# The S5 mixer's kernel product, a pair of inputs to a quarter of TensorE's columns, and its transposes at places of their own

## The chip, the cores and the metric

The kernel runs on one core of a Trainium2 chip. The metric is the device time of one execution in microseconds (us), the median of several runs. A core has a matrix engine (TensorE, in the profile PE), a vector engine (VectorE, DVE), a scalar engine (ScalarE, ACT), GpSimd (POOL) and SyncE (SP), which here only issues DMA transfers. Each engine works through its own queue of instructions in order; semaphores make one wait for another. PE reads its operands from SBUF, 128 partitions wide, and writes its results into PSUM; the output's partitions are the columns of PE.

## The reference, cut to what matters

One inference step of a two-layer streaming encoder, float32, model width 1024, 1024 prompt positions and 64 sample positions. Layer 0 mixes tokens by sliding-window attention, layer 1 by an S5 state-space model; after each mixer stands a gated ConvFFN of width 2816. The state-space model has 64 groups of 16 channels, each with 64 complex states:

```python
lbar_re, lbar_im = mag * cos(li * dt), mag * sin(li * dt)        # mag = exp(lr * dt)
bbar_re = cr[..., None] * br - ci[..., None] * bi                # and bbar_im
h[t] = lbar * h[t - 1] + bbar @ u[t]                             # complex, for each group
y = einsum('blgp,gip->blgi', sr, c_re) - einsum('blgp,gip->blgi', si, c_im) + d_skip * u
z = gelu(y);  out = (z @ w_glu + b_glu)[..., :D] * sigmoid((z @ w_glu + b_glu)[..., D:])
```

The kernel computes this over blocks of eight positions. For that it needs, for every group, the short convolution kernel K[t] = Re(C λ^t B) for t = 0 to 7 (16 × 16 channels each). This is the mixer's kernel product.

## The kernel before, in words

All large products (projections, FFN, GLU) go through `mm3` (L221): weight and input are each split into a high and a low part, and three matmuls (L223, L224, L225) add up in PSUM. A block of outputs is 128 channels by 384, 384 or 320 positions, summed over eight slices of the model width, 24 matmuls in a row. The tiles come from a framework that gives every instruction a priority in the order in which the program is written (`tc.cur_priority` counts up) and then forms each engine's queue by these priorities and a timeline of its own. `later(n)` (L118) writes the instructions inside it with a priority n lower than their place. `order(x, y)` (L112) makes x follow y in the queue.

The matrices of the state-space model are prepared while PE works on the first FFN's up-projection: `ffn` calls `aside` (L443) after each step, and in the first 32 of these (SIDE, L27) it advances the generator `ssm_prep` (L1098) by one piece under `later(LOW)` (LOW is 1500, L26). The pieces are `ssm_small`, and then for each of eight chunks q (four pairs of groups each) `ssm_chunk(q)` in two pieces and `ssm_toeplitz(q)`. A chunk:

- computes `ct` (C times powers of λ; DVE), `oc` (ACT) and `w` (B times powers of λ; six DVE instructions by `cmul`, of which L887 is the last),
- puts each group's B into `bd_` (ACT, L1048), a tile filled with zeros once,
- multiplies on PE, in float32: `kps` (L1062), eight matmuls for four pairs g and two parts c (real and imaginary). Before the change `bd_[:, g, c]` is 128 columns wide with the pair's 32 columns at 32 g and zeros beside them, and all eight matmuls add up in the same 128 × 128 of PSUM,
- takes `kps` out on DVE to `kt` (L1066, L1067), which goes to DRAM (`kd`); `ssm_toeplitz` reads it from there, rearranges it and writes it into `prm`,
- transposes `w` on PE in two groups of four, one for each part c (`wps`, L1073), takes each group out on ACT (`b3`, L1074) and writes it into `prm` too; last, POOL computes the tables `tab`.

`kps` and the transposes of part 0 share one PSUM tile (`sm0`); the transposes of part 1 have `sm1`. So the part-0 group waits until DVE has read `kps`; the part-1 group does not, and waits at most for `w` and for ACT's earlier reading. All of `kps` and `wps` are ordered behind the last product that was written when the chunk was (`behind`, L1059).

Around this, DVE works for the up-projection: it takes products out of PSUM (L411), runs the convolution (L419 to L421 on ACT and DVE), and in these turns forms sums of gated activations for the down-projection (`jt`, L370 to L373, written to DRAM as `td`).

The mixer itself, `ssm` (from L1196), comes after the FFN. It goes through 32 pairs in batches, mostly of two: `p` = U by `pm` on PE (L1249), tables on ACT, a scan on DVE (L1297), then two products into `po` (L1309 with `pm` and U, L1315 with the scan's result). `pm` is a pair of `prm`'s pairs, loaded by SP (L1213). U is the input, in four pieces of 16 groups (L1186, two DMAs each); the third and fourth stand in buffers that earlier tiles held, the third in that of the FFN's last block, so that it must wait until this block has been written out to `x1` (the spill, L1552). ACT takes `po` out and every second batch writes it to DRAM as `yd` (L1330); SP reads it back as `yf` (L1335), and ACT applies the GELU to it as `z` (L1350). SP's queue holds the spill, and all `pm`, U and `yf`, in one row.

Of the kernel before, what the change touches and what calls it, by code (L numbers as in the profile page):

```python
# [8 lines left out]
F32 = mybir.dt.float32  # L9
F32R = mybir.dt.float32r  # L10
I32 = mybir.dt.int32
AF = mybir.ActivationFunctionType
# [3 lines left out]
P = 128  # L16
# [27 lines left out]
class Core:  # L44
# [72 lines left out]
    @contextmanager  # L117
    def later(self, n):  # L118

        p = self.tc.cur_priority  # L120
        self.tc.cur_priority = p + n
        yield
        self.tc.cur_priority = p

    @contextmanager
    def boundary(self, nsq=2):
# [84 lines left out]
    behind = ()  # L211
# [680 lines left out]
    def ssm_small(self):  # L892

        nc, a = self.nc, self.a
# [5 lines left out]
        sm = self.prep.tile([P, 1024], F32, name="sm0", tag="sm").rearrange("p (a q) -> p a q", a=32)  # L900
# [79 lines left out]
        c, s = cs, sn  # L980
        for k in range(10):
# [8 lines left out]
            c, s = (ph[:, 0, k - 2], ph[:, 1, k - 2]) if k > 1 else (ta[:, 8], ta[:, 9])  # L990
# [3 lines left out]
        for t, n, p0 in ((self.tq[:, :, 0:32], 16, 0), (self.tp[:, :, 18:36], 9, 4)):  # L994
            t = t.rearrange("p q (c k) -> p q c k", c=2)
            V.memset(t[:, :, 0, 0:1], 1.0)
            V.memset(t[:, :, 1, 0:1], 0.0)
            w, k = 1, p0
            while w < n:
# [3 lines left out]
                m = [m[:, i, :NPR * u].rearrange("p (q j) -> p q j", j=u) for i in range(2)]  # L1003
                self.cmul(V, [t[:, :, i, w:w + u] for i in range(2)], [t[:, :, i, 0:u] for i in range(2)], y, m)
                w, k = w + u, k + 1
        self.bd_ = self.prep.tile([P, 4, 2, P], F32, name="bd", tag="sm")
        V.memset(self.bd_, 0.0)
        self.dv = self.prep.tile([P, 24], F32, name="dv")
        nc.sync.dma_start(self.dv[:, 16:], a["s_d"])
# [6 lines left out]
    def ssm_chunk(self, q):  # L1016

        nc, a = self.nc, self.a
        G, V = nc.gpsimd, nc.vector
        gs = slice(4 * q, 4 * q + 4)  # L1020
        if q == 0:
            z = self.pt([P, 8, 112], "z0")
            G.memset(z, 0.0)
            nc.sync.dma_start(self.kd[:, 0:7].rearrange("(b p) t i -> p b (t i)", p=P), z)
        two = lambda t, o, n: (t[:, gs, o:o + n], t[:, gs, o + n:o + 2 * n])
        (ac, as_), (bbr, bbi), (cr, ci) = (two(self.tq, o, 16) for o in (0, 32, 64))
        (pr, pi), (bc, bs) = two(self.tp, 0, 9), two(self.tp, 18, 9)

        ct = self.pt([P, 4, 2, 9, 16], "ct")
        m = self.pm2()  # L1030
        m1, m2 = (m[:, i].rearrange("p (g t i) -> p g t i", t=9, i=16) for i in range(2))
        wide = lambda x: x[:, :, None, :].to_broadcast([P, 4, 9, 16])
        tall = lambda x: x[:, :, :, None].to_broadcast([P, 4, 9, 16])
        V.tensor_mul(m1, wide(cr), tall(pr))
        V.tensor_mul(m2, wide(ci), tall(pi))
        V.tensor_sub(ct[:, :, 0], m1, m2)
        V.tensor_mul(m1, wide(cr), tall(pi))
        V.tensor_mul(m2, wide(ci), tall(pr))
        V.scalar_tensor_tensor(ct[:, :, 1], m1, -1.0, m2, op0=ALU.mult, op1=ALU.subtract)
        oc = self.pt([P, 4, 2, 16, 8], "oc")  # L1040
        for c in range(2):
            nc.scalar.activation(oc[:, :, c], ct[:, :, c, 1:9].rearrange("p g t i -> p g i t"), AF.Copy)
        nc.sync.dma_start(self.prm[:, gs, OC:OC + 256], oc.rearrange("p g c i t -> p g (c i t)"))

        for e, r in enumerate((slice(0, 64), slice(64, 128))):
            o = self.bd_[r, 0, 0, 16 * e:16 * e + 1]
            o = bass.AP(tensor=o.tensor, offset=o.offset, ap=[o.ap[0], [2 * P + 32, 4], [P, 2], [1, 16]])
            nc.scalar.activation(o, self.tq[r, gs, 32:64].rearrange("p g (c j) -> p g c j", c=2), AF.Copy)  # L1048

        w = self.pt([P, 4, 2, 16, 8], "w")  # L1050
        m = self.pm2()
        m = [m[:, i, :512].rearrange("p (g j s) -> p g j s", j=16, s=8) for i in range(2)]
        row = lambda x: x[:, :, :, None].to_broadcast([P, 4, 16, 8])
        pwr = lambda x: x[:, :, None, 0:8].to_broadcast([P, 4, 16, 8])
        self.cmul(V, (w[:, :, 0], w[:, :, 1]), (row(bbr), row(bbi)), (pwr(pr), pwr(pi)), m)
        yield

        kps = self.sm_ps("kps", 0)
        behind = self.last_mm  # L1059
        for g in range(4):  # L1060
            for c in range(2):
                x = nc.tensor.matmul(kps[:, :P], self.bd_[:, g, c], ct[:, g, c, 0:8].rearrange("p t i -> p (t i)"),  # L1062
                                     start=g + c == 0, stop=g + c == 4)
                self.order(x, behind)
        kt = self.prep.tile([P, P], F32, name="kt")
        V.scalar_tensor_tensor(kt[:, 0:16], self.dv[:, :16], self.dv[:, 16 + q:17 + q], kps[:, 0:16], op0=ALU.mult, op1=ALU.add)  # L1066
        V.tensor_copy(kt[:, 16:], kps[:, 16:P])  # L1067
        nc.sync.dma_start(self.kd[q * P:q * P + P, 7:].rearrange("j t i -> j (t i)"), kt)
        b3 = self.pt([P, 4, 2, P], "b3")
        for c in range(2):  # L1070
            wps = self.sm_ps("wps", c)
            for g in range(4):
                self.order(nc.tensor.transpose(wps[:, g * P:g * P + P], w[:, g, c].rearrange("p j s -> p (j s)"), self.ident), behind)  # L1073
            nc.scalar.activation(b3[:, :, c], wps.rearrange("p (g n) -> p g n", g=4), AF.Copy)  # L1074
        nc.sync.dma_start(self.prm[:, gs, OW:OW + 256], b3.rearrange("p g c n -> p g (c n)"))

        tab = self.pt([P, 4, 2, 144], "tab")
        m = self.pm2()
        m = [m[:, i].rearrange("p (g b a) -> p g b a", b=9, a=16) for i in range(2)]
        v = lambda i: tab[:, :, i].rearrange("p g (b a) -> p g b a", a=16)  # L1080
        self.cmul(G, (v(0), v(1)), (wide(ac), wide(as_)), (tall(bc), tall(bs)), m)
        G.tensor_copy(tab[:, :, :, 129:138], tab[:, :, :, 0:9])
        for c, o in enumerate((OCO, OSI)):
            nc.gpsimd.dma_start(self.prm[:, gs, o:o + 138], tab[:, :, c, 0:138])
# [515 lines left out]
```

## Time and profile before

| | us |
| --- | --- |
| median of 3 runs | 2254.64 |
| lowest and highest | 2249.07, 2256.94 |
| profiled execution, its own time | 2264.88 |
| its span in the trace | 2263.1 |
| PE busy | 2201.7 (97%) |
| DVE busy | 1688.5 (75%) |
| ACT busy | 1019.2 (45%) |
| eight chunks' `kps` and transposes on PE | 615.6 to 898.9 |
| the state-space model's batches, first and last `pm` issued | 1181.2 to 1278.7 |

The span is the time from the first to the last instruction in the trace of one profiled execution. A row of the timeline gives the start in us, how long the instruction was there, the engine, the line, what was written from what, the shape and how many of the kind stood in a row; in brackets stands how long the engine was idle before it, and for whom it waited. Matmuls are pipelined: a row's duration overlaps the next, so what one costs is read from the distance between the starts. Of each float32 matmul the trace has two records, of the split products (fp32r) one. In a shape such as 128*64 128x256 the first pair is rows by columns of PE.

### The profile page before, as it was taken

Reading aid. Unit: us, or ns where it says so; the run is one execution under the profiler, and the core shown is the slowest. Engines: PE = TensorE matmul, PEld = TensorE weight load, DVE = VectorE, ACT = ScalarE, POOL = GpSimd, SP = SyncE. Lnnn points to the kernel's source line nnn. Section 1 sums busy time; section 2 is a strip of 40 time slices with the busy share of each in tenths; the row PEclk is TensorE's granted clock in tenths of the full one; section 3 lists DMA queues with packets and bytes.
Section 4 is the critical chain, followed back from the end, with each engine's and each line's share of the span. In section 5 each row is a group of like instructions: output and inputs, shape, how many; then the busy total and the mean of one; then the engine's idle time right before and its main releaser. Section 6 shows DMA issues by size and latency. Waiting matters only on the chain. (4 is left out here: it accounts for less than half of the span.)

```text
span 2263.1 us, 36074 instructions
## 1 busy us (share of the span) xinstructions
PE 2201.7 (97%) x13875; PEld 2122.4 (94%) x13875; DVE 1688.5 (75%) x2954; ACT 1019.2 (45%) x1839; POOL 415.2 (18%) x474
## 2 busy tenths in 40 slices
PE   8999999999999999999998899999999999999997
PEld 8987789999999999999996799999999999989997
DVE  8677647989877777667767855588997787686764
ACT  5255747422333343455534641263544444355543
POOL 5322004200042423000200034352011011100000
PEclk9999999999999999999998999999999999999999
DMA  5100014656345565887749888652266577578773
GB/s 195 37 21 29 16 65 151 242 191 211 107 138 185 178 203 179 259 288 222 227 164 339 262 286 300 234 166 74 96 233 218 213 287 258 193 250 278 222 256 99
DMA packets 208124, 428.48 MB, mean 189 GB/s; under 512 B 23312, under 2 KB 114224, under 8 KB 205008
## 3 DMA queue, kind: packets, MB, share of 16 engines
q1 hardware_dynamic: 175648, 326.56, 44.0%
q0 software_dynamic: 23984, 95.12, 11.6%
q10 hardware_dynamic: 8320, 4.49, 0.9%
q8 instruction: 109, 1.79, 0.3%
q14 instruction: 63, 0.52, 0.1%
HBM read 297.75 MB, written 128.37 MB: 188 GB/s over the span
## 5 line engine op out<-in xcount | busy, mean ns | idle before, releaser
L223 PE MATMUL mm<-hl,whl 128*128 128x384 f32 (+1 forms) x1960 | 643.8, 329 | 7.7 <-DVE hl L306 3.1
L225 PE MATMUL mm<-hh,whl 128*128 128x384 f32 (+1 forms) x1960 | 641.1, 328 | 2.3 <-DVE whl L216 2.3
L224 PE MATMUL mm<-hh,whl 128*128 128x384 f32 (+1 forms) x1960 | 642.2, 328 | 0.0
L223 PEld LDWEIGHTS mm<-hl,whl 128*128 128x128 f32 x1960 | 368.4, 188 | 10.8 <-DVE hl L306 4.5
L225 PEld LDWEIGHTS mm<-hh,whl 128*128 128x128 f32 x1960 | 368.4, 188 | 2.9 <-DVE whl L216 2.9
L224 PEld LDWEIGHTS mm<-hh,whl 128*128 128x128 f32 x1960 | 368.7, 188 | 0.0
L216 ACT ACTIVATE whl<-raw 128x1024 fp32r<-128x1024 f32 x202 | 212.9, 1058 | 339.1 <-PE mm L225 176.4
L216 DVE TENSOR_TENSOR whl<-raw,whl 128x1024 fp32r<-128x1024 f32 x202 | 254.4, 1263 | 96.7 <-ACT whl L216 96.2
L223 PE MATMUL mm<-gt,whl 128*128 128x384 f32 (+1 forms) x968 | 318.5, 329 | 7.9 <-DVE y L613 3.6
L225 PE MATMUL mm<-gt,whl 128*128 128x384 f32 (+1 forms) x968 | 316.9, 328 | 0.7 <-DVE whl L216 0.7
L224 PE MATMUL mm<-gt,whl 128*128 128x384 f32 (+1 forms) x968 | 317.3, 328 | 0.0
L223 PEld LDWEIGHTS mm<-gt,whl 128*128 128x128 f32 x968 | 182.9, 189 | 10.5 <-DVE y L613 4.9
L225 PEld LDWEIGHTS mm<-gt,whl 128*128 128x128 f32 x968 | 182.7, 189 | 1.0 <-DVE whl L216 1.0
L224 PEld LDWEIGHTS mm<-gt,whl 128*128 128x128 f32 x968 | 182.8, 189 | 0.0
L194 DVE TENSOR_TENSOR whl<-raw,whl 128x1024 fp32r<-128x1024 f32 x84 | 96.3, 1153 | 73.0 <-ACT whl L193 72.4
L193 ACT ACTIVATE whl<-raw 128x1024 fp32r<-128x1024 f32 x84 | 82.6, 986 | 126.8 <-DMA raw<-sd 51.0
L419 ACT ACTIVATE t<-u,ppt 128x1090 f32<-128x1090 f32 x88 | 114.2, 1298 | 50.6 <-DVE u L521 24.6
L420 DVE SCALAR_TENSOR_TENSOR t<-u,ppt,t 128x1090 f32<-128x1090 f32 x88 | 123.6, 1406 | 9.8 <-ACT t L419 9.1
L421 DVE SCALAR_TENSOR_TENSOR t<-u,ppt,t 128x1090 f32<-128x1090 f32 x88 | 123.4, 1403 | 0.4
L563 DVE TENSOR_TENSOR gt<-gr,gt 128x768 fp32r<-128x768 f32 (+2 forms) x106 | 90.2, 880 | 10.7 <-ACT gt L562 10.1
L331 POOL TENSOR_TENSOR y<-y,xl 128x768 f32<-128x768 f32 (+1 forms) x16 | 31.3, 1954 | 354.0 <-DVE y L328 288.0
L562 ACT ACTIVATE gt<-gr 128x768 fp32r<-128x768 f32 (+2 forms) x106 | 78.3, 771 | 39.5 <-DMA gr<-gd 30.2
(390 smaller groups left out, 4181.0 us busy)
## 6 DMA issues: line engine op xcount, KB each, us to landing
raw<-in_w_up SPq DMA_DIRECT2D x88, 512.0 KB, 4.3
raw<-in_w_down SPq DMA_DIRECT2D x74, 512.0 KB, 4.5
raw<-sd SPq DMA_DIRECT2D x40, 512.0 KB, 4.6
sj<-in_w_up POOLq DMA_DIRECT2D x68, 256.0 KB, 6.4
su<-sj POOLq DMA_DIRECT2D x34, 512.0 KB, 5.8
raw<-su SPq DMA_DIRECT2D x34, 512.0 KB, 4.8
pm<-prm SPq DMA_DIRECT2D x32, 522.0 KB, 8.2
gr<-td SPq DMA_DIRECT2D x40, 384.0 KB, 5.9
```

What stands on the lines that cost most here:

```text
L193: nc.scalar.activation(w[:, 0], raw, AF.Copy)
L194: nc.vector.tensor_sub(w[:, 1], raw, w[:, 0].bitcast(F32))
L216: x = nc.scalar.activation(w[:, 0], raw, AF.Copy), nc.vector.tensor_sub(w[:, 1], raw, w[:, 0].bitcast(F32))
L223: nc.tensor.matmul(out, w[:, 0, sl], xl, start=start, stop=False)
L224: nc.tensor.matmul(out, w[:, 0, sl], xh, start=False, stop=False)
L225: self.last_mm = nc.tensor.matmul(out, w[:, 1, sl], xh, start=False, stop=stop)
L331: x = by[q].tensor_add(yq, yq, xs[q])
L419: nc.scalar.activation(t, u[:, 0:T + 2], AF.Identity, bias=cb(m), scale=cw(0, m))
L420: nc.vector.scalar_tensor_tensor(t, u[:, 1:T + 3], cw(1, m), t, op0=ALU.mult, op1=ALU.add)
L421: self.last_conv = nc.vector.scalar_tensor_tensor(t, u[:, 2:T + 4], cw(2, m), t, op0=ALU.mult, op1=ALU.add)
L562: nc.scalar.activation(x[:, 0, u], raw, AF.Copy)
L563: nc.vector.tensor_sub(x[:, 1, u], raw, x[:, 0, u].bitcast(F32))
```

## The change

`bd_` becomes 32 columns wide: each pair's weights alone, without the zeros for the other pairs. Each of the eight `kps` matmuls writes only its pair's 32 partitions of PSUM, so that a pair takes a quarter of PE's columns. The loop over the parts c is now the outer one, and each pair adds up over c by itself. A new context manager `due(p)` writes an instruction with the priority p itself instead of one relative to its place. The eight `kps` all get the priority that the place of the first has; the transposes of part 1 get that plus 12, and are now written first; those of part 0 get it plus 50.

```diff
+    @contextmanager
+    def due(self, p):
+
+        q = self.tc.cur_priority
+        self.tc.cur_priority = p
+        yield
+        self.tc.cur_priority = q
...
-        self.bd_ = self.prep.tile([P, 4, 2, P], F32, name="bd", tag="sm")
+        self.bd_ = self.prep.tile([P, 4, 2, 32], F32, name="bd", tag="sm")
...
         for e, r in enumerate((slice(0, 64), slice(64, 128))):
-            o = self.bd_[r, 0, 0, 16 * e:16 * e + 1]
-            o = bass.AP(tensor=o.tensor, offset=o.offset, ap=[o.ap[0], [2 * P + 32, 4], [P, 2], [1, 16]])
-            nc.scalar.activation(o, self.tq[r, gs, 32:64].rearrange("p g (c j) -> p g c j", c=2), AF.Copy)
+            nc.scalar.activation(self.bd_[r, :, :, 16 * e:16 * e + 16], self.tq[r, gs, 32:64].rearrange("p g (c j) -> p g c j", c=2), AF.Copy)
...
-        for g in range(4):
-            for c in range(2):
-                x = nc.tensor.matmul(kps[:, :P], self.bd_[:, g, c], ct[:, g, c, 0:8].rearrange("p t i -> p (t i)"),
-                                     start=g + c == 0, stop=g + c == 4)
+
+        due = self.tc.cur_priority
+        for c in range(2):
+            for g in range(4):
+                with self.due(due):
+                    x = nc.tensor.matmul(kps[32 * g:32 * g + 32, :P], self.bd_[:, g, c], ct[:, g, c, 0:8].rearrange("p t i -> p (t i)"),
+                                         start=c == 0, stop=c == 1)
                 self.order(x, behind)
...
-        for c in range(2):
+        for c in (1, 0):
             wps = self.sm_ps("wps", c)
             for g in range(4):
-                self.order(nc.tensor.transpose(wps[:, g * P:g * P + P], w[:, g, c].rearrange("p j s -> p (j s)"), self.ident), behind)
+                with self.due(due + (50 if c == 0 else 12)):
+                    x = nc.tensor.transpose(wps[:, g * P:g * P + P], w[:, g, c].rearrange("p j s -> p (j s)"), self.ident)
+                self.order(x, behind)
```

What this does to the queues is seen in their order. PE's queue, chunk 0 in the up-projection, before (`mm` are the FFN's products, `whl` its weights; the eight `kps` go on alternating with products, and nine products after the last stands the first transpose):

```order
L224 MATMUL mm<-hh,whl 128x384
L225 MATMUL mm<-hh,whl 128x384
L1062 MATMUL kps<-ct,bd 128x128
L223 MATMUL mm<-hl,whl 128x320
L1062 MATMUL kps<-ct,bd 128x128
L224 MATMUL mm<-hh,whl 128x320
L1062 MATMUL kps<-ct,bd 128x128
L225 MATMUL mm<-hh,whl 128x320
```

The same place now, where the lines stand some eight to ten further down:

```order
L232 MATMUL mm<-hh,whl 128x384
L233 MATMUL mm<-hh,whl 128x384
L1071 MATMUL kps<-ct,bd 32x128
L231 MATMUL mm<-hl,whl 128x320
L1071 MATMUL kps<-ct,bd 32x128 x7
L232 MATMUL mm<-hh,whl 128x320
L233 MATMUL mm<-hh,whl 128x320
```

One `kps` still has a product behind it; the other seven stand together. Eleven products after them comes one transpose of part 1, a product, and the other three; before, the group's four stood alternating with products. The part-0 group stands some twenty products further on, likewise one, a product, three; before, in one run of four, seven products after the other group.

DVE's queue, the fifth chunk (`w` its last product, `kt` the way out of `kps`, `jt` and `u` the FFN's), before:

```order
L887 TENSOR_TENSOR w<-m 128x4x128
L371 TENSOR_TENSOR jt<-jt 128x384
L411 TENSOR_TENSOR u<-rb,mm 128x384
L372 TENSOR_TENSOR jt<-jt 128x384
L373 TENSOR_TENSOR jt<-jt 128x384
L1066 SCALAR_TENSOR_TENSOR kt<-dv,kps 128x16
L1067 COPY kt<-kps 128x112
L411 TENSOR_TENSOR u<-rb,mm 128x256
```

And now:

```order
L895 TENSOR_TENSOR w<-m 128x4x128
L379 TENSOR_TENSOR jt<-jt 128x384
L419 TENSOR_TENSOR u<-rb,mm 128x384
L380 TENSOR_TENSOR jt<-jt 128x384
L1075 SCALAR_TENSOR_TENSOR kt<-dv,kps 128x16
L1076 COPY kt<-kps 128x112
L381 TENSOR_TENSOR jt<-jt 128x384
L419 TENSOR_TENSOR u<-rb,mm 128x256
```

`kt` stands ahead of the last of the sums instead of behind it. The same holds in the third and the seventh chunk; in the eighth it moved ahead of an L411; the others are unchanged. `w` keeps its place.

SP's queue in the state-space model's stage, where the change touches no line, before (`pm` are loads of pairs of `prm`, U_11629 the third piece of the input and U_11888 the fourth, `x1` the spill):

```order
L1213 DMA pm_11601<-prm_289 128x1044 x2
L1552 DMA x1_91<-y_10702 1024x1x320
L1213 DMA pm_11691<-prm_289 128x1044 x2
L1186 DMA U_11629<-hd_10753 128x8x137 x2
L1213 DMA pm_11748<-prm_289 128x1044 x2
L1335 DMA yf_11747<-yd_11538 128x1096
L1213 DMA pm_11804<-prm_289 128x1044 x2
L1213 DMA pm_11861<-prm_289 128x1044 x2
L1186 DMA U_11888<-hd_10753 128x8x137 x2
L1335 DMA yf_11860<-yd_11538 128x1096
L1213 DMA pm_11932<-prm_289 128x1044 x2
```

And now:

```order
L1224 DMA pm_11601<-prm_289 128x1044 x2
L1563 DMA x1_91<-y_10702 1024x1x320
L1197 DMA U_11629<-hd_10753 128x8x137 x2
L1224 DMA pm_11691<-prm_289 128x1044 x2
L1224 DMA pm_11748<-prm_289 128x1044 x2
L1346 DMA yf_11747<-yd_11538 128x1096
L1224 DMA pm_11804<-prm_289 128x1044 x2
L1224 DMA pm_11861<-prm_289 128x1044 x2
L1346 DMA yf_11860<-yd_11538 128x1096
L1197 DMA U_11888<-hd_10753 128x8x137 x2
L1224 DMA pm_11932<-prm_289 128x1044 x2
```

The third piece of the input stands ahead of the load of pairs 12 and 13 (pm_11691), and the second `yf` ahead of the fourth piece. On PE two of this stage's L1309 groups stand behind the next batch's `p` instead of ahead of it. ACT's and POOL's queues change by single neighbouring places.

## Prediction

> **What bounds the kernel now.** The page first: section 1 says which engine fills the span.
>
> ```profile
> span 2263.1 us, 36074 instructions
> PE 2201.7 (97%) x13875; PEld 2122.4 (94%) x13875; DVE 1688.5 (75%) x2954; ACT 1019.2 (45%) x1839; POOL 415.2 (18%) x474
> ```
>
> TensorE (PE) is busy for 97% of the span. So an instruction taken from its queue shortens the time by what it holds that queue, and a wait taken from another engine only where PE waits for it. Next the list of PE's waits (total, times, longest), of which three belong to the places that the change touches.
>
> ```profile
> PE p L1249 <- DMA pm<-prm: 4.8, 5, 2.1
> ...
> PE wps L1073 <- DVE kt L1067: 4.4, 3, 1.7
> ...
> PE wps L1073 <- DVE w L887: 2.9, 3, 1.2
> ```
>
> The two L1073 rows are the chunk's transposes, which wait for VectorE (DVE): one group for `w`, the other for `kt`, whose read frees the PSUM tile they share with `kps`. The L1249 row is in the SSM stage. Then the timeline of PE in chunk 0, where it is not disturbed by waits.
>
> ```profile
> 615.62 0.38 PE L1062 MATMUL kps<-ct,bd 128*128 128x128 f32 x2
> ...
> 618.58 0.31 PE L225 MATMUL mm<-hh,whl 128*128 128x320 f32 x1
> ...
> 619.75 0.27 PE L1073 MATMUL wps<-ident,w 128*128 128x128 f32 x1
> ...
> 620.78 0.30 PE L225 MATMUL mm<-hh,whl 128*128 128x320 f32 x1
> ```
>
> From 618.58 to 619.75 eight products of 320 columns run: 1.17 us, 0.146 each from start to start. From 615.62 to 618.58 eight `kps` and eight products alternate: 2.96 − 1.17 = 1.79 us for the eight `kps`, 0.22 each; each is two records, so 0.11 a record. From 619.75 to 620.78 four transposes alternate with four products: 1.03 − 4 × 0.146 = 0.45, 0.11 each. At full width an instruction costs its own columns and nothing for standing between others.
>
> **The kps in quarters.** Each chunk's eight `kps` now write 32 partitions each, so they use 32 of the columns of PE. No row of before shows four quarters. The nearest shows halves: the attention's `po`, 64 columns wide, among full-width products.
>
> ```profile
> 232.55 0.31 PE L225 MATMUL go<-oh,whl 128*128 128x320 f32 x1
> 232.79 0.65 PE L796 MATMUL po<-ptT,vt 128*64 128x256 f32 x4
> 233.37 0.33 PE L789 MATMUL tps<-ident,ptT 128*128 128x128 f32 x1
> ...
> 261.11 1.09 PE L796 MATMUL po<-ptT,vt 128*64 128x256 f32 x8
> 262.13 0.41 PE L223 MATMUL go<-ol,whl 128*128 128x320 f32 x1
> 262.38 0.31 PE L224 MATMUL go<-oh,whl 128*128 128x320 f32 x1
> ```
>
> Four records take 0.58 (232.79 to 233.37), eight take 1.02: 0.44 for four more, 0.11 each, although a record of 256 columns alone should take twice the 0.11 of one of 128. So two halves run at once, 0.22 a pair, and 0.58 − 0.44 = 0.14 a run is left over. The last full-width product ahead holds 0.24 instead of 0.146 (232.55 to 232.79), the first behind 0.25 (262.13 to 262.38): 0.09 and 0.10 more. Leaving full width and coming back costs 0.14 + 0.09 + 0.10 = 0.33 us an excursion.
>
> By the order, the eight do not stand in one run: one comes first, then a product, then seven. That is two excursions. The lone one costs 2 × 0.11 + 0.33 = 0.55. Of the seven, no quarter holds more than two (four records): 4 × 0.11 + 0.33 = 0.77 if all four quarters run at once. Together 1.32 against 1.79: −0.47 a chunk, **−3.8 us** for eight. If only two run at once, the seven take 0.88 + 0.33 = 1.21, together 1.76: −0.2 in all. If none, 14 × 0.11 + 0.33 = 1.87, together 2.42: +5.0 in all. I take four at once, since the halves show nothing but full concurrency.
>
> The rule that speaks against this change: the Trainium skill, TensorEngine Tiling (Array Packing), section Key Properties, says that changing the tiling mode (not just the tile) drains TensorE. It names no price; the trace agrees, with 0.33 an excursion, and without it the term would be 1.79 − 0.66 = 1.13 a chunk, −9.0 in all. The Trainium skill, TensorE: Matmul & The Clock Gate, Part 3 (packing small matmuls), measures 2.38× for three column tiles instead of 3×; by that an estimate of the seven's 0.44 is 0.55, and the term −2.9.
>
> **The waits of the transposes.** Before, the group that waits for `w` stood behind 16 products and the eight `kps`, 16 × 0.146 + 1.79 = 4.13 us after the chunk's first `kps`. Now 12 products and the shorter `kps` are ahead of it: 1.75 + 1.32 = 3.07. `w` does not come sooner by that. Two of the eight chunks, the fifth (PE, then DVE) and the last:
>
> ```profile
> 772.36 0.38 PE L1062 MATMUL kps<-ct,bd 128*128 128x128 f32 x2
> 781.65 0.63 PE L1073 MATMUL wps<-ident,w 128*128 128x128 f32 x4 [1.44 <-DVE kt L1067]
> 777.13 0.69 DVE L887 TENSOR_TENSOR w<-m 128x512 f32<-128x512 f32 x1
> 779.77 1.41 DVE L373 TENSOR_TENSOR jt<-jt 128x384 f32<-128x384 f32 x1
> 781.11 0.22 DVE L1066 SCALAR_TENSOR_TENSOR kt<-dv,kps 128x16 f32<-128x16 f32 x1
> ...
> 890.61 0.38 PE L1062 MATMUL kps<-ct,bd 128*128 128x128 f32 x2
> 895.54 0.68 DVE L887 TENSOR_TENSOR w<-m 128x512 f32<-128x512 f32 x1
> ```
>
> In the fifth, `w` ends at 777.82, 5.5 after the first `kps`; in the last at 896.22, 5.6 after. Over the eight chunks the same subtraction gives −6.5, 2.5, 2.3, 4.8, 5.5, 3.6, 3.8, 5.6. Set against 4.13 (the last chunk's products are partly 384 wide, its place 4.4) the waits are 0.7, 1.4 and 1.3, in all 3.4; set against 3.1 (in the last chunk 4.7, since its order changes more) they are 1.7, 2.4, 0.6, 0.7 and 1.0, in all 6.4: **+3.0 us**. These are delays of the queue, a little more than the 2.9 of idle time in the waits' list.
>
> The group that waits for `kt` moves the other way, from six to eight products after the other group to some twenty. And in the third, fifth and seventh chunk DVE now does `kt` ahead of L373 (1.41 us, above) instead of behind it. Its delays before were 1.85, 1.7 and 1.4 (second, fifth, seventh chunk; 4.9 in all). The last two go, and so does what they would have hidden; the second chunk's falls to 1.1, as PE is about 0.75 later there. **−3.9 us.** What is late next is L373 in three chunks, by the 0.35 of `kt`; its `jt` goes out to DRAM for the down-projection, which has not begun. `bd` written by simpler ScalarE instructions: as many, off the path, 0. The smaller fill with zeros (DVE) runs once, ahead of the first chunk: 0.
>
> Sum in the up-projection: −3.8 + 3.0 − 3.9 = −4.7. With no concurrency of quarters PE comes later, the `w` delays are 1.9 and the `kt` delays 0: +5.0 − 1.5 − 4.9 = −1.4.
>
> **The SSM stage.** The changed priorities also move two loads on SP's queue there; nothing is added. These are SP's issues before, then PE's `p` batches, then ACT's `z`.
>
> ```profile
> DMA packets 23980, 37.55 MB, mean 289 GB/s; under 512 B 1040, under 2 KB 17424, under 8 KB 23968
> ...
> U<-hd SPq DMA_DIRECT2D x8, 548.0 KB, 9.7
> ```
> ```profile
> 1212.13 0.52 SPq L1552 DMA_DIRECT2D x<-y  x1
> 1215.06 4.60 SPq L1213 DMA_DIRECT2D pm<-prm  x2
> 1225.87 1.11 SPq L1186 DMA_DIRECT2D U<-hd  x2
> 1227.10 5.55 SPq L1213 DMA_DIRECT2D pm<-prm  x2
> ...
> 1237.87 1.80 SPq L1186 DMA_DIRECT2D U<-hd  x2
> 1247.57 0.33 SPq L1335 DMA_DIRECT2D yf<-yd  x1
> ```
> ```profile
> 1226.68 1.16 PE L1249 MATMUL p<-U,pm 128*64 128x137 f32 x16
> ...
> 1231.77 1.16 PE L1249 MATMUL p<-U,pm 128*64 128x137 f32 x16
> ...
> 1239.32 0.69 PE L1249 MATMUL p<-U,pm 128*64 128x137 f32 x8 [0.70 <-DMA pm<-prm]
> ...
> 1250.65 1.16 PE L1249 MATMUL p<-U,pm 128*64 128x137 f32 x16
> ...
> 1257.88 0.69 PE L1249 MATMUL p<-U,pm 128*64 128x137 f32 x8 [2.08 <-DMA pm<-prm]
> ...
> 1267.96 1.16 PE L1249 MATMUL p<-U,pm 128*64 128x137 f32 x16
> ```
> ```profile
> 1240.84 2.04 ACT L1350 ACTIVATE z<-yf 128x1024 f32<-128x1024 f32 x1 [5.08 <-DMA yf<-yd]
> ...
> 1256.51 2.04 ACT L1350 ACTIVATE z<-yf 128x1024 f32<-128x1024 f32 x1 [7.72 <-DMA yf<-yd]
> ```
>
> First move: the third `U` pair, which the queue holds until the spill of `x` has landed (1225.87), now stands ahead of the `pm` that went out at 1215.06. So this `pm` (pairs 12 and 13) goes out at about 1227 instead, where before the next one stood, and that one reached PE only at 1239.32. Its batch, which ran at 1231.77, then runs near 1239.3, and the next, a batch's 5.1 us later (1226.68 to 1231.77), at 1244.4 instead of 1239.3: +5.1. The spill may land sooner with less beside it, which would make it 0. ACT waits 5.08 for `yf` at that place anyway, so I take half: **+2.5**.
>
> Second move: `yf` now stands ahead of the fourth `U` pair. Before, it reached ACT at 1256.51, 8.9 us after its issue, with 1.1 MB of `U` issued ahead, 3.8 us at 289 GB/s. The two batches from 1250.65 to 1267.96 take 17.3 us where two undisturbed ones take 10.2: 7.1 to be had at most. Against it, the `pm` for which PE waits at 1257.88 now comes behind `U`: up to +3.8. I take half of the 7.1, **−3.5**. Together −1.0, between −7.1 and +8.9.
>
> **The sum.** −4.7 − 1.0 = −5.7. The profiled execution took 2264.88 us, 1.8 more than its span, 10.2 above the median; differences carry over: 2264.9 − 5.7 = 2259.2 there, 2254.64 − 5.7 = **2249.0** as median. A measurement of this kernel can tell about 0.3%, 6.8 us, from no change, so this alone counts as the same.
>
> **The rivals.**
> - *Relief on the queues.* `yf` ahead of `U` gives back all 7.1, since `yd`'s writes too no longer share the DMA engines with `U`. For it: the 7.72 of ACT's wait, the longest above. Against it: PE there waits for `pm` too. −4.7 + 2.5 − 7.1 = −9.3: 2245.3.
> - *SP's queue becomes the bound*, slower: `pm` behind the held `U` keeps its whole 5.1 and `pm` behind the fourth `U` its 3.8, so −4.7 + 8.9 = +4.2: 2258.8. It decides once PE's wait for `pm` in the list grows from 4.8 beyond 9.5, the 4.7 gained. For it: PE waits for `pm` already. Against it: as many bytes move, and ACT and the spill have slack.
> - *The quarters do not run at once*: the change does not do what it says, −1.4 − 1.0 = −2.4: 2252.2. Against it: the halves do.
>
> **How the numbers follow.** Forecast 0.45, of which 0.20 beyond 0.3% faster (its 5.7 lies just inside the 6.8) and 0.25 within. Relief 0.22: 0.20 faster, 0.02 same. SP's queue 0.20: 0.12 slower (the median of three has itself a spread of 8 us), 0.08 same. Quarters 0.08: 0.06 same, 0.02 slower. Unforeseen 0.05: 0.02 faster, 0.03 slower. In all 0.42, 0.41, 0.17. The range goes from relief with another 4 us (half the runs' spread), 2241, to SP's case with a little more, 2260.
>
> **What would show it.** In the profile after: the lone `kps` near 0.55 and the seven near 0.77 from start to start (right), or 1.2 or 1.9 (fewer at once); the `w` row near 6 and the `kt` row near 1; in the SSM stage the `p` batch of pairs 12 and 13 near 1239 and `z` sooner than 1256. The prediction is wrong if the `kps` hold more than 1.8 a chunk, if `w` comes earlier as well, or if the stage from 1195 to 1310 changes by more than 7 us.

## The result, and the profile after

The changed kernel takes 2261.49 us (median of 14 runs, 2257.29 to 2267.67), the kernel before 2253.15 (14 runs, 2245.65 to 2258.04): a ratio of 1.0037, 95% interval 1.0025 to 1.0049. It is slower by some 8 us, where 5.7 us less was forecast and a range up to 2260.0 given.

The first lines of the page after, and the three rows of its list of PE's waits that answer to those shown of before:

```profile
span 2257.3 us, 36086 instructions
PE 2195.0 (97%) x13875; PEld 2108.0 (93%) x13875; DVE 1687.0 (75%) x2954; ACT 1019.7 (45%) x1839; POOL 413.8 (18%) x474
```
```profile
PE p L1260 <- DMA pm<-prm: 9.4, 6, 3.0
PE wps L1083 <- DVE w L895: 6.1, 6, 1.7
...
PE wps L1083 <- DVE kt L1076: 1.3, 1, 1.3
```

The rows look as forecast for the transposes (6.1 for `w`, 1.3 for `kt`), and the wait for `pm` has doubled. Yet this span is 5.8 us *shorter* than the one of before, while the medians say 8 us longer. The profiled execution of before took 2264.88 us, more than any of its 14 runs: a reader of two traces alone would have the sign wrong. So the same kernel was traced again (label again, below). The same rows of that trace:

```profile
span 2254.2 us, 36074 instructions
```
```profile
PE p L1249 <- DMA pm<-prm: 4.8, 4, 2.2
...
PE wps L1073 <- DVE kt L1067: 3.0, 2, 1.5
...
PE wps L1073 <- DVE w L887: 1.4, 2, 0.9
```

Against this one, PE waits longer after the change: 4.6 us more for `pm`, 4.7 more for `w`, 1.7 less for `kt`.

PE in chunk 0, after:

```profile
614.89 0.34 PE L233 MATMUL mm<-hh,whl 128*128 128x384 f32 x1
615.15 0.41 PE L1071 MATMUL kps<-ct,bd 128*32 128x128 f32 x2
615.49 0.41 PE L231 MATMUL mm<-hl,whl 128*128 128x320 f32 x1
615.84 0.64 PE L1071 MATMUL kps<-ct,bd 128*32 128x128 f32 x14
616.40 0.42 PE L232 MATMUL mm<-hh,whl 128*128 128x320 f32 x1
616.66 0.30 PE L233 MATMUL mm<-hh,whl 128*128 128x320 f32 x1
```

From 614.89 to 616.66 are 1.77 us, of which three products at their own pace would take 0.174 + 2 × 0.146 = 0.47. The eight `kps` hold PE 1.30 us; 1.32 was forecast, 1.79 was the time before. The seven alone, fourteen records, stand 0.56 from start to start: four quarters do run at once.

### The profile page after: what moved, and what is told of

Read it like the earlier page. It is cut to its first block, busy times and chain, and to the rows that moved or that the text cites. A ratio compares the mean times of both kernels' runs of the same rounds, so it can differ in the third digit from the quotient of the medians.

```text
span 2257.3 us, 36086 instructions
## 1 busy us (share of the span) xinstructions
PE 2195.0 (97%) x13875; PEld 2108.0 (93%) x13875; DVE 1687.0 (75%) x2954; ACT 1019.7 (45%) x1839; POOL 413.8 (18%) x474
## 3 DMA queue, kind: packets, MB, share of 16 engines
q8 instruction: 109, 1.79, 0.3%
## 5 line engine op out<-in xcount | busy, mean ns | idle before, releaser
L419 DVE TENSOR_TENSOR u<-rb,mm 128x384 f32<-128x384 f32 (+1 forms) x164 | 80.1, 501 | 20.4 <-PE mm L233 15.6
```

The source lines that it names most:

```text
L419: nc.vector.tensor_mul(u[:, t0 + 2:t0 + 2 + np_], rb[:, t0:t0 + np_], ps[:, :np_])
```

## The experiments

Ratios are to the kernel before, timed on the same chip in the same call; 0.1% is 2.3 us. "Back" means an order of before restored by dependences or priorities, with all other queues as in the kernel it is built on, unless said otherwise.

**again**: the kernel before, no edit.

> The kernel before, unchanged, for a second trace of it: the first trace's execution (2264.88 us) is longer than all 14 timed runs of it (2245.65 to 2258.04). Every theory expects a ratio of 1.000. Where the 8.3 us of the change come from must show in this trace: if it is the state-space stage, the stage from 1180 to 1320 is some 10 us shorter here than in the first trace; if it is the up-projection, 590 to 910 is; if neither, the first trace's excess lies elsewhere and the change's loss too.

Measured: 0.9997 (0.9985 to 1.0009). The second trace is 8.9 us shorter than the first; 7.3 of it lie between the chunks' first `kps` and the last product of the down-projection (568.7 and 561.4 us), in code that is the same in both. So waits of one execution are a sample: 7.3 us at the transposes in the first trace, 4.4 here, and 4.5, 5.4 and 3.3 in the traces of sp_fwd, sp_move1 and sp_move2 (below), all five the same code up to there.

**sp_back**: the kernel after, with both moves on SP's queue in the state-space stage back.

```diff
                 if qs[0] == 2:
                     self.order(self.spill(), self.last_u)
-                    us.append(self.ssm_load(2))
+                    us.append(None)
...
                     load(t + 5, got[4])
+                    if t == 1:
+                        us[2] = self.ssm_load(2)
+                        self.order(self.first_u, got[6])
+                        self.order(self.last_u, got[6])
...
                     yfs.append(x)
+                    if kt == 1:
+                        self.order(x, self.last_u)
```

> The kernel after, with the two moved loads on SyncE's queue in the state-space stage put back (third input piece behind the load of pairs 12 and 13, second yf behind the fourth piece); all other queues as in the kernel after. Theory A, the moved loads cost the time: 1.0037 falls to about 0.998 (the up-projection's -4.7 alone). Theory B, the loss is made in the up-projection (quarters or transposes): stays at 1.003 to 1.004. Theory C, half and half: about 1.001.

Measured: 1.0022 (1.0006 to 1.0038). Of 8.3 us the moves carry about 3.4, by the two intervals together anything from −1 to 8; what is left over the kernel before is clear of zero, so a part is elsewhere.

**full_width**: the kernel after with the product over all columns again, the places as changed; the scheduler leaves the state-space stage as before, moves some neighbours on DVE, ACT and SP in the up-projection, and in the last chunk puts `td` ahead of `prm<-b` and the `gr` loads ahead of `tl` (these names are explained below). Cut from the diff: the ACT instructions that fill `bd_`, which go back too.

```diff
-        self.bd_ = self.prep.tile([P, 4, 2, 32], F32, name="bd", tag="sm")
+        self.bd_ = self.prep.tile([P, 4, 2, P], F32, name="bd", tag="sm")
...
-                    x = nc.tensor.matmul(kps[32 * g:32 * g + 32, :P], self.bd_[:, g, c], ct[:, g, c, 0:8].rearrange("p t i -> p (t i)"), start=c == 0, stop=c == 1)
+                    x = nc.tensor.matmul(kps[:, :P], self.bd_[:, g, c], ct[:, g, c, 0:8].rearrange("p t i -> p (t i)"), start=g + c == 0, stop=g + c == 4)
```

> The kernel after with the kernel product at full width again (zeros in bd), but with the change's priorities and places; the scheduler then leaves the loads of the state-space stage as before. Theory A (moved loads): about 0.999 (the places alone: w waits a little longer, kt waits gone). Theory B with the quarters as the cost (drains that the timeline does not show): 0.999 as well, told from A by sp_back. Theory B with the places as the cost: 1.003 or more.

Measured: 1.0047 (1.0033 to 1.0061). The places without the quarters are no better than with them, and the state-space stage stands as before here: so the places, with what the scheduler moved for them, cost. Where they may, shows at the end of the up-projection. SP's queue there, in the second trace of before (`kd` is the last chunk's `kt` going out, `prm<-b` its transposed `w`, `tl` the loads that bring `kt` back from `kd`, `td` the last sums going out, `gr` the first loads of the down-projection):

```profile
894.44 0.78 SPq L1068 DMA_DIRECT2D kd<-kt  x1
...
897.04 0.58 SPq L1075 DMA_DIRECT2D prm<-b  x1
903.33 5.10 SPq L1094 DMA_DIRECT2D tl<-kd  x8
908.53 0.53 SPq L374 DMA_DIRECT2D td<-jt  x1
909.16 1.51 SPq L574 DMA_DIRECT2D gr<-gd  x2
```

The same in the kernel after:

```profile
895.75 0.46 SPq L1077 DMA_DIRECT2D kd<-kt  x1
...
899.94 0.37 SPq L1086 DMA_DIRECT2D prm<-b  x1
906.39 0.33 SPq L382 DMA_DIRECT2D td<-jt  x1
906.88 7.66 SPq L1105 DMA_DIRECT2D tl<-kd  x8
914.65 1.12 SPq L582 DMA_DIRECT2D gr<-gd  x2
```

SP's queue changed here too, which neither the part on the change nor the prediction takes up: `td` stands ahead of `tl`. It needs the last of DVE's sums, for which SP waits 4.5 us in after, and `tl` goes out only behind it. The part-0 transposes, now some two dozen products further back than before, add to this: `prm<-b`, which needs them and ACT's reading, goes out 4.2 us behind `kd` instead of 2.6. The eight `tl` then take 7.66 us to issue instead of 5.10; why was not isolated. The last of them is out 18.8 us after `kd` instead of 14.0.

ACT's queue passes this on. ACT turns `tl` into `tp`, and behind this stand the FFN's next weights (`whl`, which DVE finishes) and ACT's and DVE's part of `gt`, from which PE makes the first product of the down-projection. ACT's row for `tp` in the second trace of before, in after and in full_width:

```profile
910.39 2.01 ACT L1095 ACTIVATE tp<-tl 128x1024 f32<-128x1024 f32 x1 [14.48 <-DMA tl<-kd]
```
```profile
916.44 2.02 ACT L1106 ACTIVATE tp<-tl 128x1024 f32<-128x1024 f32 x1 [16.52 <-DMA tl<-kd]
```
```profile
926.49 2.00 ACT L1108 ACTIVATE tp<-tl 128x1024 f32<-128x1024 f32 x1 [10.28 <-DMA tl<-kd]
```

That is 15.9, 20.7 and 29.9 us behind the last chunk's `kd`, and DVE then stands 0.9, 7.1 and 10.1 us for ACT's `whl`. PE's first product of the down-projection, in the traces of after and of full_width:

```profile
931.11 0.44 PE L231 MATMUL mm<-gt,whl 128*128 128x384 f32 x1 [0.49 <-DVE gt L571]
```
```profile
936.43 0.69 PE L231 MATMUL mm<-gt,whl 128*128 128x384 f32 x1 [3.73 <-DVE gt L571]
```

In the second trace of before no such wait stands there. That it is `tl` and not the late `gr`, from which `gt` is made, full_width tells: there `gr` went out 12.4 us behind `kd` (896.55), sooner than before, and PE waited longest:

```profile
908.96 2.80 SPq L582 DMA_DIRECT2D gr<-gd  x2
914.21 10.25 SPq L1107 DMA_DIRECT2D tl<-kd  x8
```

**width**: the kernel before with the quarters alone. Cut from the diff: the ACT instructions that fill `bd_`, as in the change.

```diff
-        self.bd_ = self.prep.tile([P, 4, 2, P], F32, name="bd", tag="sm")
+        self.bd_ = self.prep.tile([P, 4, 2, 32], F32, name="bd", tag="sm")
...
-                x = nc.tensor.matmul(kps[:, :P], self.bd_[:, g, c], ct[:, g, c, 0:8].rearrange("p t i -> p (t i)"), start=g + c == 0, stop=g + c == 4)
+                x = nc.tensor.matmul(kps[32 * g:32 * g + 32, :P], self.bd_[:, g, c], ct[:, g, c, 0:8].rearrange("p t i -> p (t i)"), start=c == 0, stop=c == 1)
```

> The kernel before with quarters alone, none of the priorities: the eight kps then stand one by one between products, so each is an excursion of its own. At 0.55 to 0.6 us each a chunk's eight hold PE 4.4 to 4.8 us instead of 1.79, +21 to +24 in eight chunks, less the waits of the transposes that this hides (up to 8): ratio about 1.006. If leaving full width were free, the ratio would be at or below 1.000.

Measured: 1.0079 (1.0063 to 1.0094), 18 us. The eight `kps` hold PE 4.25 us a chunk in its trace, 2.46 more than before, 19.7 in all; its waits for `w` and `kt` are gone from the list. The scheduler also made the second of the two moves in the state-space stage here, which is small beside this (sp_move2, below). Leaving full width for one `kps` at a time is as dear as the rows of `po` had said; the run of seven is what makes the quarters pay.

**last_early**: the kernel after, the last chunk's part-0 transposes seven products behind its part-1 group again; with that `td` goes out behind `tl` again.

```diff
-                with self.due(due + (50 if c == 0 else 12)):
+                with self.due(due + (50 if c == 0 and q < 7 else 12)):
```

> The kernel after, with one thing undone: in the last of the eight chunks the part-0 transposes stand seven products behind the part-1 group again (as before the change) instead of some thirty, and the sums td go out behind the tl loads again. Theory L, the late transposes of the last chunk hold SyncE's queue (their prm write stands ahead of the tl and gr loads) and so delay the start of the down-projection: the gr loads go out some 5 us sooner than in the kernel after, PE's waits for gt at 930 go, and 1.0037 falls by 3 to 6 us, to 1.001 to 1.0025. Theory S, the state-space stage alone makes the loss: stays within 1 us of 1.0037.

Measured: 1.0017 (1.0004 to 1.0031). SP's queue at the same place:

```profile
898.45 0.78 SPq L1077 DMA_DIRECT2D kd<-kt  x1
...
901.56 0.55 SPq L1086 DMA_DIRECT2D prm<-b  x1
907.97 5.11 SPq L1105 DMA_DIRECT2D tl<-kd  x8
913.17 0.53 SPq L382 DMA_DIRECT2D td<-jt  x1
913.80 1.51 SPq L582 DMA_DIRECT2D gr<-gd  x2
```

The last `tl` is out 14.6 us behind `kd` and `gr` 15.4, close to before, ACT's `tp` begins 16.5 behind it, and no wait for `gt` is left. The time falls by 4.5 us, by the two intervals together some 0.5 to 8.5: within theory L's range, with `tl` rather than `gr` as the load that matters. Transposes and `td` went back together, so what each of them costs stays open.

**both_back**: last_early and sp_back together.

> The kernel after, with the last chunk's transposes early (as in last_early) and the two moved loads of the state-space stage put back (as in sp_back). If both theories hold, what is left is the gain of the quarters and of the kt waits less the w waits: 0.998 to 0.9995. If the places of the transposes cost time in every chunk, it stays above 1.001.

Measured: 0.9998 (0.9987 to 1.0008). The two losses add: 1.0022 falls by 0.0024 with the last chunk back, 1.0017 by 0.0019 with SP's moves back, both clear of zero. But what is left is no change, not the gain that was expected. Its waits at the transposes are as long as in the kernel after:

```profile
PE wps L1083 <- DVE w L895: 5.9, 6, 1.6
...
PE p L1260 <- DMA pm<-prm: 2.7, 3, 2.0
```

**sp_fwd**: the kernel before with nothing but the two moves. **sp_move1** and **sp_move2**: one of them each.

```diff
-                    load(t + 5, got[4])
+                    load(t + 5, self.last_u if t == 1 else got[4])     # first move
...
-                    us.append(self.ssm_load(3))                        # second move
+                    us.append(None)
...
                     yfs.append(x)
+                    if kt == 1:
+                        us[3] = self.ssm_load(3)
+                        self.order(self.first_u, x)
+                        self.order(self.last_u, x)
```

> The kernel before, with nothing but the two moves on SyncE's queue in the state-space stage. From sp_back against the kernel after (2258.0 against 2261.5) theory S expects +3.5 us, 1.0015, with a lower mean clock (waits of PE in a stage in which its clock is halved already). If the moves are neutral: 1.000. If yf ahead of the fourth piece brings what the prediction said, 0.9995.

> The kernel before, with the first move on SyncE's queue alone: the third input piece, held until the spill has landed, ahead of the load of pairs 12 and 13. The prediction took +2.5 (0 to 5.1) for it, ratio 1.001; if it makes the whole loss of sp_fwd (1.0015), 1.0015 or more.

> The kernel before, with the second move alone: the second yf ahead of the fourth input piece. The prediction took -3.5 (-7.1 to +3.8), ratio 0.9985. sp_fwd's 1.0015 with move 1 at +2.5 would leave +1 for it: 1.0005. If the load behind the fourth piece comes late: 1.0015.

Measured: both 1.0015 (1.0003 to 1.0028), the first alone 1.0011 (0.9998 to 1.0025), the second alone 1.0008 (0.9996 to 1.0020). The moves cost 3.4 us, the same from either side (sp_back, sp_fwd; by itself only the second is clear of zero). Of the single moves neither is clear of zero, and their sum fits. The gain forecast for the second, 0.9985, lies outside its interval. PE's wait for `pm` in sp_fwd, and in sp_move2:

```profile
PE p L1249 <- DMA pm<-prm: 7.0, 4, 3.6
```
```profile
PE p L1249 <- DMA pm<-prm: 7.4, 7, 3.4
```

In the two traces of before it is 4.8, in sp_back 5.1, in both_back 2.7. The kernel after shows what happens, first SP's issues, then ACT's `z`, then PE's batches:

```profile
1244.54 0.32 SPq L1346 DMA_DIRECT2D yf<-yd  x1
1245.03 2.04 SPq L1197 DMA_DIRECT2D U<-hd  x2
1247.24 3.14 SPq L1224 DMA_DIRECT2D pm<-prm  x4
```
```profile
1248.66 2.11 ACT L1361 ACTIVATE z<-yf 128x1024 f32<-128x1024 f32 x1 [1.95 <-DMA yf<-yd]
```
```profile
1231.78 0.69 PE L1260 MATMUL p<-U,pm 128*64 128x137 f32 x8 [2.23 <-DMA pm<-prm]
...
1256.88 0.71 PE L1260 MATMUL p<-U,pm 128*64 128x137 f32 x8 [2.39 <-DMA pm<-prm]
```

`yf` does reach ACT 4.1 us after its issue instead of 8.9, and ACT's wait of 7.72 has become 1.95. PE gets nothing from it: its batch waits for `pm`, and this went out 2.7 us behind `yf` (1247.24 against 1244.54), with the fourth piece ahead of it, instead of 0.5 (1248.06 against 1247.57 in the first trace of before). The first of the two PE rows is the batch of pairs 12 and 13, of the first move: it runs 7.4 us behind the batch before it (1224.39) instead of 5.1.

**w_late**: both_back, with the part-1 transposes of the first seven chunks back at the part-0 group, where `w` is there.

```diff
-                with self.due(due + (50 if c == 0 and q < 7 else 12)):
+                with self.due(due + (12 if q == 7 else 50)):
```

> both_back (0.9998), with the part-1 transposes of the first seven chunks moved back to the part-0 group, 31 to 37 products behind the chunk's first kps instead of 12, so that w is there when PE comes to them. Theory W, the gain of the quarters is eaten by PE standing at these transposes for w (some 6 to 7 us of waits in the traces, about 1 of them in the last chunk): the w waits fall to about 1 and the ratio to 0.997 to 0.998. Theory X, the quarters gain nothing: stays at 0.9995 or above.

Measured: 0.9995 (0.9983 to 1.0008). The waits changed their name:

```profile
PE wps L1083 <- DVE kt L1076: 6.1, 4, 2.4
...
PE wps L1083 <- DVE w L895: 1.2, 1, 1.2
```

7.3 us instead of 6.5 in both_back. Theory W, that PE could cash the quarters by reading `w` later, is not borne out.

**w_late_full**: w_late at full width.

> w_late with the kernel product at full width again (zeros in bd), nothing else meant to move (a few neighbours in the vector engine's and the scalar engine's queues do). With the waits gone the quarters' own price must show: by the rows, 1.79 us a chunk against 1.30, 0.49 each, +3.9 us against w_late. If the quarters gain nothing by themselves: the same as w_late.

Measured: 1.0038 (1.0024 to 1.0052), 9.7 us above w_late where 3.9 was expected. The trace has 11.5 us of waits for `kt` and two stretches of halved clock in the up-projection; the scheduler moved parts of DVE's and SP's queues too. The sign is as expected, the price of the quarters cannot be read from it.

**all_late**: w_late, with the part-0 group of the first seven chunks 19 products further back.

```diff
-                with self.due(due + (12 if q == 7 else 50)):
+                with self.due(due + (12 if q == 7 else 70 if c == 0 else 50)):
```

> w_late (0.9995) with the part-0 transposes of the first seven chunks another 19 products further back (50 to 56 behind the chunk's first kps), so that kt is there too; the scheduler then also moves jt, td and prm transfers by some places. Theory P, PE alone paces the up-projection and its waits (6.1 us for kt, 1.2 for w in w_late's trace) are what is left to gain: both rows fall to 1 to 2 us together and the ratio to 0.996 to 0.9975. Theory D, the vector engine paces it too, and an earlier PE only waits elsewhere (w and kt came later after the first kps the earlier PE was: 3.9 to 6.8 us in w_late against 2.8 to 4.7 in the kernel after): stays at 0.999 to 1.000, with waits of the products in place of the transposes'.

Measured: 1.0043 (1.0026 to 1.0059). Neither theory: the wait for `kt` is gone, and in two chunks `w` is late instead, after the scheduler had also moved `jt`'s and `td`'s transfers and others that stand between them on SP's queue, and DVE's work in many places.

```profile
PE wps L1083 <- DVE w L895: 12.4, 2, 7.2
```

No version faster than the kernel before came out; both_back and w_late equal it.

## Why the prediction was wrong, step by step

- **The quarters**: right. 1.32 us a chunk forecast, 1.30 measured, −3.9 us of PE's queue; the price of an excursion (width) and four at once hold.
- **The waits of the transposes**: the directions were right, the sizes not. Over the five traces whose queues are alike up to there (before, again, sp_fwd, sp_move1, sp_move2) the waits for `w` are 2.9, 1.4, 0.4, 1.2 and 1.3 and for `kt` 4.4, 3.0, 4.1, 4.2 and 2.0; over after, sp_back, last_early and both_back 6.1, 7.1, 9.5 and 5.9, and 1.3, 0.8, 1.2 and 0.6. In the means `w` grew by 5.7 (forecast 3.0), `kt` fell by 2.6 (forecast 3.9). With the quarters' −3.9 that is −0.8 instead of −4.7, and both_back, in which little else is left than neighbouring places in the queues, measures −0.5 us (−2.9 to +1.8). The failed assumption is "`w` does not come sooner by that", taken to mean that it does not come later either. In the third to eighth chunk `w` ended on average 3.6 us after the chunk's first `kps` over the five traces, and 4.5 over the four. The prediction had also read `w` off the first trace alone, where in the fourth and fifth chunk it came 4.8 and 5.5 us after; in the other four traces it is 2.1 to 3.1. It looks as if DVE and its transfers kept a pace of their own, and PE stood at the transposes for what it had saved ahead of them: w_late moved the place and PE stood for `kt`. That DVE sets the pace of this stage fits these runs; what exactly holds its `w` and `kt` was not isolated.
- **The last chunk** was the missing term. The prediction priced the part-0 group's later place on PE and DVE alone ("What is late next is L373") and took SP's queue as changed in the state-space stage only. Here `prm<-b` goes out later and `td` stands ahead of `tl`, and ACT's and DVE's work for the down-projection stands behind `tl`. last_early against after is −4.5 us, both_back against sp_back −5.4: that the last chunk's order costs this is shown. The path through `tl` and ACT is read from single traces, and these show less than the 4.5: PE is on the edge there, with a wait of 0.49 us in one execution of after, 0 in the one of sp_back, and 3.73 in full_width, where the clock halved for 6.8 us as well. That the 4.5 is a mean over such executions is argued, not shown.
- **The first move in the state-space stage**: +2.5 forecast, 1.0011, that is +2.5, measured, with an interval from −0.5 to +5.6. That the batch of pairs 12 and 13 comes late was right, by 2.3 us in the trace of after where 5.1 had been read; to take half of the 5.1 was a choice, and that it fits so well is in part luck.
- **The second move**: −3.5 forecast, +1.8 measured (−0.9 to +4.5). `yf` came sooner as forecast, but it was ACT's wait (7.72 in the first trace of before), and PE's batch waited for `pm`. The 7.1 us of which the prediction gave `yf` a half were not its to give: in that trace PE stood still for 3.6 us of them, 2.6 of this for `pm` (2.08 and 0.48), and for 6.8 us the clock was at half, which is about the rest. Its rival, `pm` behind the fourth piece, was the right mechanism.

Together −0.5 + 4.5 + 3.4 = +7.4 of the 8.3 measured; the rest is within the intervals. The slower rival had 3.8 of its 8.9 from this, and counted on −4.7 that did not come.

## What to carry to other kernels

Work that is made shorter ahead of a wait for another engine can be paid back at the wait; before it is counted, ask whether the other engine's result would be there sooner. When a scheduler or a changed priority moves an instruction, follow its result, and whatever the scheduler moved with it, through the queues behind it, at the last repetition of the loop above all, where the next stage's first loads stand behind it. And take two traces of the kernel before: one execution's waits may differ by more than the change is worth.

## What the runs showed of the hardware

The clock had a part in the loss; how large a part, the runs do not tell. The mean granted clock over the runs was 0.9892 for the kernel after (14 runs) and 0.9916 for the kernel before (23 runs, the first call): 1.08% of 2261.6 us against 0.84% of 2253.4, 24.4 us against 18.9 that would be lost if PE worked through all the time at half clock: at most 5.5 of the 8 us. For sp_fwd it was 0.9897 against 0.9912 of the kernel before in its call, 23.3 us against 19.9: at most 3.4 us, as much as the two moves cost. But PE stands still for part of that time, and loses nothing by the clock while it does. How a wait brings a low clock about is seen in all_late: the transposes wait 7.16 us, from 774.8 to 781.9 (PE's row, then busy time by stretches, with the granted clock third from the end):

```profile
781.92 1.11 PE L1083 MATMUL wps<-ident,w 128*128 128x128 f32 x4 [7.16 <-DVE w L895]
```
```profile
770.00:776.00 6.00, 4.77 (x30) 4.44 (x28) 3.95 (x8) 3.48 (x5) 0.00 (x0) 1.00 0.81 254
776.00:780.00 4.00, 0.00 (x0) 0.00 (x0) 4.00 (x8) 1.16 (x2) 0.00 (x0) 0.60 0.19 78
780.00:790.00 10.00, 8.08 (x36) 8.03 (x37) 9.41 (x13) 4.08 (x8) 4.91 (x3) 0.65 0.40 147
790.00:796.00 6.00, 6.00 (x40) 6.00 (x39) 1.89 (x3) 1.06 (x1) 5.49 (x6) 1.00 0.64 205
```

The clock is at half for 10.2 us, from 776.8 to 787.0. PE works only for the last 5.1 of them, so there the clock itself costs some 2.6 us, half of what the mean clock would say. The Trainium skill, TensorE: Matmul & The Clock Gate, Part 1, says that the clock halves after an idle window of some 3.4 us and comes back after a busy one, and that these windows run freely. The coming back, 5.1 us after the wait has ended, agrees with this. The halving does not: it came 2.0 us into the wait, when PE could not yet have been idle for a whole such window; in full_width it came 2.3 us into the wait of 3.73. In the state-space stage, too, the mean granted clock of after is 0.89 from 1180 to 1320 (0.90 in both traces of before), and no wait of PE that stands in its list there is longer than 3.0 us. So shorter waits are enough, and what a wait will cost by the clock could not be told from its length.
